# The first FFN's up products: nine of 22 pairs by seven half-size products each

## The chip, the cores and the metric

The kernel runs on one core of one Trainium2 chip. The metric is device microseconds of one launch, from the inputs in HBM to the output in HBM, as the median of several runs.

## The reference

A decoder trunk of two layers works on 512 tokens of width 1024 in float32. Layer 0 mixes the tokens by gated linear attention, layer 1 by a short gated convolution, and each is followed by a convolutional FFN:

```
def conv_ffn(h, w_up, conv_w, w_down):
    up = causal_dwconv(h @ w_up, conv_w)          # (512, 1024) @ (1024, 5632), 3 taps
    a, u = up[..., :D_FF], up[..., D_FF:]         # D_FF = 2816
    return (jax.nn.silu(a) * u) @ w_down          # (512, 2816) @ (2816, 1024)
for i in range(2):
    x = x + mixer_i(rmsnorm(x, norm_mix_g[i]))
    x = x + conv_ffn(rmsnorm(x, norm_ffn_g[i]), w_up[i], conv_w[i], w_down[i])
return rmsnorm(x, final_norm_g)
```

Only the FFN of layer 0 is touched by the change.

## The kernel before, in words

Activations lie transposed: channels on the 128 partitions, 512 tokens along the free axis. `x[0]` to `x[7]` are the residual stream, 128 channels each. Every float32 product is made of three matmuls in the reduced format fp32r: a value is split into a high part (a rounding copy) and a low part (the rest), and `mm3` (L267) multiplies high by high, high by low and low by high into one PSUM bank. The activation's parts are `xparts[k]`; the weight's parts are made on the way in.

Weights come through class `Weights` (L80). A source of 128 x 1024 is loaded by SyncE into one of 4 raw slots (`wraw`). `part` (L151) splits it by `halve` (L118) into one of 3 slots `wh`, `wl`: ScalarE copies the high part, VectorE subtracts it. `take` (L179) is called once per weight unit; it starts a load, lets `part` prepare the unit two ahead, and returns the one that is due. `group` (L274) takes units and runs 24 matmuls for an up unit of 1024 columns.

The program is written with a tile framework which places instructions on each engine's queue at build time and inserts the waits.

The first FFN is `ffn_blocks(0, 1, 2)` (L649). It goes through `ff_steps` (L196). An up step `("up", j)` computes channel block j of the `a` half and of the `u` half (two groups of 24 matmuls of 512 columns), multiplies each by the row factor `r` (L676), applies the three-tap convolution (`conv3`, L328: one ScalarE scaling and two shifted VectorE multiply-adds), SiLU on `a`, the product (L679) and a split into `gp[j]` (L680). The 22 blocks are cut into four (`BLOCKS`: 6, 5, 5 and 6). From the second block on, an up step is followed by one or two down products of the block before, `("dn", b, m)`: 15 or 18 matmuls of 512 columns, added to `x[m]` on VectorE (L656). The eight down products of the last block come at the end. Step 0 also makes `r` (sums of squares, a root, and a reciprocal on VectorE, L325).

The list `SEVEN` (L31) names up steps that are done by Strassen's method in Winograd's form: the pair of channel blocks, the two halves of the 1024 inputs and the two halves of the tokens make a 2 x 2 times 2 x 2 block product, which takes seven half-size products instead of eight. It is empty, so that none of `sums`, `forms`, `seven_forms` (L592), `product` (L608) and `up_seven` (L616) is run. `seven_forms` makes the four sums of activation blocks for one of four pairs of tiles; where `SEVEN` is not empty it runs after steps 1 to 4.

Of the kernel before, what the change touches and what calls it, by code (L numbers as in the profile page):

```python
# [11 lines left out]
F32R = mybir.dt.float32r  # L12
AF = mybir.ActivationFunctionType
ALU = mybir.AluOpType

P = 128
T = 512
D = 1024
KD = D // P
# [8 lines left out]
WARM = 10  # L28
DOWN_CUTS = ((0, 8), (8, 16), (16, 22))
BLOCKS = ((0, 6), (6, 11), (11, 16), (16, 22))  # L30
SEVEN = ()  # L31


@with_exitstack
def trunk_kernel(ctx, tc, xT, w_qk, w_v, w_g, w_up_gate, b_gate, w_go, w_sc, w_so, w_up, w_dn,
# [2 lines left out]
    V, S, G, PE = nc.vector, nc.scalar, nc.gpsimd, nc.tensor  # L38

    const = ctx.enter_context(tc.tile_pool(name="const", bufs=1))  # L40
    wraw = ctx.enter_context(tc.tile_pool(name="wraw", bufs=4))
    wsp = ctx.enter_context(tc.tile_pool(name="wsp", bufs=3))
    work = ctx.enter_context(tc.tile_pool(name="work", bufs=2))
    big = ctx.enter_context(tc.tile_pool(name="big", bufs=1))
    tiny = ctx.enter_context(tc.tile_pool(name="tiny", bufs=2))
# [2 lines left out]
    def ps(name):  # L48
        return psp.tile([P, T], F32, tag="ps", name=name)
# [8 lines left out]
    def bt(tag, name, shape=(P, T), dt=F32):  # L58
        return big.tile(list(shape), dt, tag=tag, name=name)
# [20 lines left out]
    class Weights:  # L80
# [13 lines left out]
            self.units.append(None)  # L94

        def add_pair(self, a, b):
            n, i = len(self.srcs), len(self.units)
            self.srcs += [a, b]
            self.paired.add(n + 1)
            self.last += [i + 3, i + 2]  # L100
            self.need += [n + 1] * 4
            self.units += [(n, q) for q in range(4)]

        def load(self, between=lambda: None):
            if self.nl < len(self.srcs):
                src = self.srcs[self.nl]
                r = wraw.tile([P, UNIT], F32, tag="wraw", name=f"wr{self.nl}")
                n = src.shape[1]
                step = (UNIT // 4, UNIT // 2, UNIT)[min(self.nl, 2)]
                for c in range(0, n, step):  # L110
                    nc.sync.dma_start(r[:, c:min(c + step, n)], src[:, c:min(c + step, n)])
                    between()
                self.raw[self.nl] = r[:, :n]
                self.nl += 1
                if self.nl - 1 in self.paired:
                    self.sums(self.nl - 2)

        def halve(self, hh, ll, src):  # L118
            S.copy(hh, src)  # L119
            V.tensor_sub(ll, src, hh.bitcast(F32))  # L120

        def sums(self, n):

            ra, rb = self.raw[n], self.raw[n + 1]
            lo, hi = slice(0, T), slice(T, 2 * T)
            s = bt(f"b13{'hl'[self.npair % 2]}", f"s{n}")
            self.npair += 1
            nc.sync.dma_start(s, self.srcs[n + 1][:, lo])
            G.dma_start(rb[:, lo], rb[:, hi], accum_op=ALU.add)
            G.dma_start(s, ra[:, lo], accum_op=ALU.add)  # L130
            self.third[n] = s

        def forms(self, n, q, h, l):


            ra, rb = self.raw[n], self.raw[n + 1]
            lo, hi = slice(0, T), slice(T, 2 * T)
            if q == 0:
                self.halve(h[:, lo], l[:, lo], ra[:, lo])
                G.dma_start(ra[:, lo], rb[:, lo], accum_op=ALU.add)  # L140
                self.halve(h[:, hi], l[:, hi], self.third.pop(n))
            elif q == 1:
                self.halve(h[:, hi], l[:, hi], ra[:, hi])
                G.dma_start(ra[:, hi], ra[:, lo], accum_op=ALU.add)
                self.halve(h[:, lo], l[:, lo], ra[:, lo])
            elif q == 2:
                self.halve(h, l, rb)
            else:
                self.halve(h[:, lo], l[:, lo], ra[:, hi])

        def part(self):  # L151
            if self.ns < len(self.units):
                while self.nl <= self.need[self.ns]:
                    self.load()
                tiles = self.hold.pop(self.ns, lambda: None)()
                pair = self.units[self.ns]
                if not tiles:
                    h = wsp.tile([P, UNIT], F32R, tag="wh", name=f"wh{self.ns}")
                    l = wsp.tile([P, UNIT], F32R, tag="wl", name=f"wl{self.ns}")
                if pair:  # L160
                    self.forms(pair[0], pair[1], h, l)
                    self.split[self.ns] = (h, l)
                    self.ns += 1
                    return
                r = self.raw.pop(self.need[self.ns])
                n = r.shape[1]
                whole = 8 <= self.ns < 16
                step = UNIT // 2 if tiles else (UNIT // 4, UNIT // 2, UNIT)[min(self.ns, 2)]
                blocks = []
                for i, c in enumerate(range(0, n, step)):  # L170
                    e = min(c + step, n)
                    hh, ll = tiles[i] if tiles else (h[:, c:e], l[:, c:e])
                    hh, ll = hh[:, :e - c], ll[:, :e - c]
                    self.halve(hh, ll, r[:, c:e])
                    blocks += [(hh[:, b:b + P], ll[:, b:b + P]) for b in range(0, e - c, P)]
                self.split[self.ns] = (h, l) if whole else blocks
                self.ns += 1

        def take(self):  # L179

            for _ in range(2):
                if self.nl < len(self.srcs) and (self.nl < 4 or self.last[self.nl - 4] < self.ns):
                    self.load()
                    if self.nl not in self.paired:
                        break
            self.part()
            self.ng += 1
            return self.split.pop(self.ng - 1)
# [7 lines left out]
    def ff_steps():  # L196
        steps = [("up", j) for j in range(*BLOCKS[0])]
        for b in range(1, len(BLOCKS)):
            n = BLOCKS[b][1] - BLOCKS[b][0]
            for i, j in enumerate(range(*BLOCKS[b])):  # L200
                steps.append(("up", j))
                steps += [("dn", b - 1, m) for m in range(KD * i // n, KD * (i + 1) // n)]
        return steps + [("dn", len(BLOCKS) - 1, m) for m in range(KD)]

    for st in ff_steps():
        if st[0] == "dn":
            a, b = BLOCKS[st[1]]
            W.add(w_dn[0, st[2]][:, a * P:b * P])
        elif st[1] in SEVEN:
            W.add_pair(w_up[0, 2 * st[1]], w_up[0, 2 * st[1] + 1])  # L210
        else:
            W.add(w_up[0, 2 * st[1]])
            W.add(w_up[0, 2 * st[1] + 1])
# [399 lines left out]
                PE.matmul(out, lhsT=a, rhs=b, start=first and k == 0 and i == 0, stop=k == 3 and i == 2,  # L613
                          skip_group_check=not first)

    def up_seven(j, tf):  # L616

        lo, hi = slice(0, HT), slice(HT, T)
        cut = lambda ks, c: [tuple(p[:, c] for p in xparts[k]) for k in ks]
        b11, b21, b22 = cut(range(4), lo), cut(range(4, 8), lo), cut(range(4, 8), hi)  # L620
        t1, t2, t3, t4 = tf
        half = lambda w, c: (w[0][:, c * T:(c + 1) * T], w[1][:, c * T:(c + 1) * T])
        n = "hl"[j % 2]
        sa, sb = bt(f"b11{n}", "sa"), bt(f"b12{n}", "sb")
        A, C = ps("upa")[:, 0:HT], ps("upc")[:, 0:HT]
        w = take()
        product(A, half(w, 0), b11, True)
        S.copy(sa[:, lo], A)
        product(C, half(w, 1), t3, True)
        S.copy(sa[:, hi], C)  # L630
        w = take()
        product(A, half(w, 0), t2, False)
        S.copy(sb[:, lo], A)
        B = ps("upb")[:, 0:HT]
        product(B, half(w, 1), b21, True)
        w = take()
        product(A, half(w, 0), t1, False)
        S.copy(sb[:, hi], A)
        product(C, half(w, 1), t4, False)
        w = take()  # L640
        product(A, half(w, 0), b22, False)
        us = [wk("u", bufs=3) for _ in range(2)]
        V.tensor_add(us[0][:, lo], sa[:, lo], B)
        V.tensor_sub(us[1][:, lo], C, sb[:, lo])
        V.tensor_sub(us[1][:, hi], sa[:, hi], sb[:, hi])
        S.copy(us[0][:, hi], A)
        return us

    def ffn_blocks(l, gi, gnext):  # L649
        gp, r, tf = {}, None, [[], [], [], []]  # L650
        V.tensor_scalar_mul(neg, vec[:, gi * KD:(gi + 1) * KD], -1.0)
        for st in ff_steps():
# [6 lines left out]
                    norm_squares(m)  # L659
                continue  # L660
            j = st[1]
            if j in SEVEN:
                us = up_seven(j, tf)
                for u in us:
                    V.tensor_mul(u, u, r)
            else:
                ups = [group("up0", xparts)]
                if j == 0:
                    sums = sum_parts(acc[0])
                ups.append(group("up1", xparts))  # L670
                if j == 0:
                    r = inv_rms_rows(sums, D)
                    y = wk("y", tag="acc", bufs=1)
                us = [wk("u", bufs=3) for _ in range(2)]
                for u, up in zip(us, ups):
                    V.tensor_mul(u, up, r)  # L676
# [165 lines left out]
```

## Time and profile before

| | |
|---|---|
| median of 3 runs (range) | 1117.98 us (1117.41 to 1118.01) |
| the profiled execution | 1118.37 us, of which the span is 1116.6 us |
| busy: PE, weight load | 1107.2 us (99%), 921.7 us (83%) |
| busy: VectorE, ScalarE, GpSimd | 695.6 us (62%), 460.8 us (41%), 5.1 us |
| granted TensorE clock, mean | 0.997 |
| instructions on PE, VectorE, ScalarE | 5020, 887, 618 |
| HBM traffic | 105.23 MB read, 2.10 MB written |
| first FFN in the span | 211.1 to 570.6 us |

The profile is one execution of the program, taken by the hardware profiler. Its times count from the start of the span. PE is TensorE's matmuls, PEld its weight loads, DVE VectorE, ACT ScalarE, POOL GpSimd, SP SyncE. Matmuls overlap in the pipeline, so that the duration of one is longer than the step from one to the next; what one costs is read from a piece of many. Durations on DVE also reach a little over the start of the next instruction.

### The profile page before, as it was taken

The numbers are of one execution on the slowest core, as the hardware profiler recorded it, in microseconds if no ns is written. First come the engines' busy times: TensorE is split into PE (matmuls) and PEld (weight loads), VectorE is DVE, ScalarE is ACT, GpSimd is POOL, SyncE is SP. The second block draws the span as 40 slices with busy tenths as digits, with TensorE's granted clock in tenths as the row PEclk, the third lists the DMA queues.
The fourth block names the chain that finished last, engine by engine and source line by source line (L and its number), as shares of the span: only waits on it lengthen the run. The fifth ranks groups of instructions, "written<-read, shape, count | busy, mean of one in ns | idle before, by whom it ended". The sixth has DMA issues, their size and how long they took to land.

```text
span 1116.6 us, 12578 instructions
## 1 busy us (share of the span) xinstructions
PE 1107.2 (99%) x5020; PEld 921.7 (83%) x5020; DVE 695.6 (62%) x887; ACT 460.8 (41%) x618; POOL 5.1 (0%) x18
## 2 busy tenths in 40 slices
PE   9999999999999999999999999999999999999997
PEld 7888888888888888888888888888888888888887
DVE  7864675597656566556666555558777777743232
ACT  6565664454333333333442222334444444432241
POOL 1000000000000000000000000000000000000000
PEclk9999999999999999999999999999999999999998
DMA  7232213222332233232332222223332222333312
GB/s 251 83 102 69 73 60 114 95 95 85 98 96 93 92 96 104 90 112 81 108 118 94 95 94 95 95 95 96 101 105 95 95 95 95 90 104 87 102 52 76
DMA packets 34334, 108.14 MB, mean 97 GB/s; under 512 B 3746, under 2 KB 6562, under 8 KB 34276
## 3 DMA queue, kind: packets, MB, share of 16 engines
q1 hardware_dynamic: 34276, 107.34, 29.8%
q8 instruction: 39, 0.64, 0.2%
q14 instruction: 19, 0.16, 0.0%
HBM read 105.23 MB, written 2.10 MB: 96 GB/s over the span
## 4 chain that ended last, share of the span: by engine, by line
PE 99%; DMA 0%; DVE 0%; ACT 0%; SPq 0%; issue 0%; DVEq 0%
PE up L272 43%; PE dn L272 20%; PE g L272 4%; PE v L272 4%; PE so L272 4%; PE scb L272 4%; PE scc L272 4%; PE scu L272 4%; PE go L272 4%; PE k L272 2%; PE q L272 2%; PE dn7b L272 1%; PE dn7a L272 1%; PE o L493 1%; PE o L495 0%; DMA x<-in_xT 0%
## 5 line engine op out<-in xcount | busy, mean ns | idle before, releaser
L119 ACT CAST wh<-wr 128x1024 fp32r<-128x1024 f32 (+4 forms) x209 | 206.3, 988 | 409.3 <-PE up L272 120.6
L120 DVE TENSOR_TENSOR wl<-wr,wh 128x1024 fp32r<-128x1024 f32 (+4 forms) x209 | 238.8, 1143 | 96.0 <-ACT wh L119 94.3
L272 PE MATMUL up<-xh,wh 128*128 128x512 f32 x704 | 273.9, 389 | 0.0
L272 PE MATMUL up<-xl,wh 128*128 128x512 f32 x704 | 273.9, 389 | 0.0
L272 PE MATMUL up<-xh,wl 128*128 128x512 f32 x704 | 273.9, 389 | 0.0
L272 PEld LDWEIGHTS up<-xh,wh 128*128 128x128 f32 x704 | 132.1, 188 | 27.7
L272 PEld LDWEIGHTS up<-xh,wl 128*128 128x128 f32 x704 | 132.1, 188 | 27.3
L272 PEld LDWEIGHTS up<-xl,wh 128*128 128x128 f32 x704 | 132.1, 188 | 27.3
L676 DVE TENSOR_TENSOR u<-up,r 128x512 f32<-128x512 f32 x44 | 30.2, 690 | 90.5 <-PE up L272 90.5
L333 DVE SCALAR_TENSOR_TENSOR c<-u,ffcw,c 128x510 f32<-128x510 f32 x88 | 65.7, 749 | 2.8
L332 DVE SCALAR_TENSOR_TENSOR c<-u,ffcw,c 128x511 f32<-128x511 f32 x88 | 65.3, 745 | 1.1 <-ACT c L331 0.8
L331 ACT ACTIVATE c<-u,ffcw 128x512 f32<-128x512 f32 x88 | 63.0, 720 | 4.1 <-DVE u L676 3.4
L585 DVE TENSOR_TENSOR u<-up,r 128x512 f32<-128x512 f32 x44 | 30.1, 687 | 37.3 <-PE up L272 37.2
L656 DVE TENSOR_TENSOR x<-x,dn 128x512 f32<-128x512 f32 x32 | 21.9, 684 | 16.9 <-PE dn L272 16.9
L587 ACT ACTIVATE c<-c 128x512 f32<-128x512 f32 x22 | 13.9, 632 | 41.9 <-DVE c L333 41.9
L325 DVE RECIPROCAL r<-r 128x512 f32<-128x512 f32 x8 | 26.8, 3351 | 4.7 <-ACT r L324 4.7
L678 ACT ACTIVATE c<-c 128x512 f32<-128x512 f32 x22 | 13.9, 632 | 37.7 <-DVE c L333 37.6
L308 ACT ACTIVATE sq<-x 128x512 f32<-128x512 f32 x34 | 21.0, 624 | 12.6 <-DVE x L716 10.9
L272 PE MATMUL g<-xh,wh 128*128 128x512 f32 x64 | 25.6, 400 | 0.0
L272 PE MATMUL v<-wh,xh 128*128 128x512 f32 x64 | 25.3, 395 | 0.0
L272 PE MATMUL g<-xh,wl 128*128 128x512 f32 x64 | 25.0, 390 | 0.0
L272 PE MATMUL v<-wh,xl 128*128 128x512 f32 x64 | 24.9, 390 | 0.0
(803 smaller groups left out, 1933.5 us busy)
## 6 DMA issues: line engine op xcount, KB each, us to landing
wr<-in_w_up SPq DMA_DIRECT2D x88, 512.0 KB, 3.3
wr<-in_w_sc SPq DMA_DIRECT2D x24, 512.0 KB, 3.3
wr<-in_w_dn SPq DMA_DIRECT2D x24, 384.0 KB, 3.0
wr<-in_w_dn SPq DMA_DIRECT2D x16, 512.0 KB, 3.5
wr<-in_w_dn SPq DMA_DIRECT2D x16, 320.0 KB, 2.8
wr<-in_w_v SPq DMA_DIRECT2D x8, 512.0 KB, 3.4
wr<-in_w_g SPq DMA_DIRECT2D x8, 512.0 KB, 3.4
wr<-in_w_go SPq DMA_DIRECT2D x8, 512.0 KB, 3.3
```

The costliest lines, as they stand in the source:

```text
L119: S.copy(hh, src)
L120: V.tensor_sub(ll, src, hh.bitcast(F32))
L272: PE.matmul(out, lhsT=a, rhs=b, start=first and i == 0, stop=last and i == 2)
L308: S.activation(sq, x[k], AF.Square)
L325: V.reciprocal(r, r)
L331: S.activation(c, u, AF.Copy, scale=cw[:, 2:3])
L332: V.scalar_tensor_tensor(c[:, 1:], u[:, :T - 1], cw[:, 1:2], c[:, 1:], op0=ALU.mult, op1=ALU.add)
L333: V.scalar_tensor_tensor(c[:, 2:], u[:, :T - 2], cw[:, 0:1], c[:, 2:], op0=ALU.mult, op1=ALU.add)
L585: V.tensor_mul(u, ups[i], r)
L587: S.activation(cs[0], cs[0], AF.Silu)
L656: V.tensor_add(x[m], x[m], part)
L676: V.tensor_mul(u, up, r)
```

## The change

`SEVEN` becomes nine of the 22 steps: 7, 9, 10, 12, 14, 15, 17, 19 and 21. Such a step is cut in two, `("s1", j)` and `("s2", j)`, with the first of its down products between them, the others (none or one) behind. `seven_first` runs four of the products (units q0 and q1 of the pair), `seven_last` three (q2 and q3). Each product is 12 matmuls (4 weight blocks, 3 terms) of 256 columns. Two PSUM banks hold them by halves; sums that several outputs share are accumulated in place, and three ScalarE copies and five VectorE operations of 256 columns make the two outputs.

The weight sums were meant for GpSimd's accumulating DMA; they are now four VectorE additions of 512 columns, in `forms`, between the splits of q0 and q1. A pair's weights stay in two raw slots from q0 to q3, a sum in `b13`, and q2's parts in tiles of their own (`b11`, `b12`). There are 6 raw slots instead of 4, and 4 slots of `wh`, `wl` instead of 3. The scratch memory for DMA descriptors is set to 1024.

```
-SEVEN = ()
+SEVEN = (7, 9, 10, 12, 14, 15, 17, 19, 21)
...
-    wraw = ctx.enter_context(tc.tile_pool(name="wraw", bufs=4))
-    wsp = ctx.enter_context(tc.tile_pool(name="wsp", bufs=3))
+    wraw = ctx.enter_context(tc.tile_pool(name="wraw", bufs=6))
+    wsp = ctx.enter_context(tc.tile_pool(name="wsp", bufs=4))
...
             if q == 0:
-                self.halve(h[:, lo], l[:, lo], ra[:, lo])
-                G.dma_start(ra[:, lo], rb[:, lo], accum_op=ALU.add)
-                self.halve(h[:, hi], l[:, hi], self.third.pop(n))
+                s3 = bt(f"b13{'hl'[n % 4 // 2]}", f"s{n}")
+                V.tensor_add(s3, ra[:, lo], rb[:, lo])
+                self.halve(h[:, lo], l[:, lo], s3)
+                V.tensor_add(rb[:, lo], rb[:, lo], rb[:, hi])
+                self.halve(h[:, hi], l[:, hi], rb[:, lo])
             elif q == 1:
-                self.halve(h[:, hi], l[:, hi], ra[:, hi])
-                G.dma_start(ra[:, hi], ra[:, lo], accum_op=ALU.add)
-                self.halve(h[:, lo], l[:, lo], ra[:, lo])
+                self.halve(h, l, ra)
+                V.tensor_add(ra[:, lo], ra[:, lo], rb[:, lo])
+                V.tensor_add(ra[:, hi], ra[:, hi], ra[:, lo])
             elif q == 2:
-                self.halve(h, l, rb)
+                self.halve(h, l, rb[:, hi])
             else:
-                self.halve(h[:, lo], l[:, lo], ra[:, hi])
+                self.halve(h, l, ra)
...
-                if self.nl < len(self.srcs) and (self.nl < 4 or self.last[self.nl - 4] < self.ns):
+                if self.nl < len(self.srcs) and (self.nl < 6 or self.last[self.nl - 6] < self.ns):
...
-                steps.append(("up", j))
-                steps += [("dn", b - 1, m) for m in range(KD * i // n, KD * (i + 1) // n)]
+                dn = [("dn", b - 1, m) for m in range(KD * i // n, KD * (i + 1) // n)]
+                steps += [("s1", j), dn[0], ("s2", j)] + dn[1:] if j in SEVEN else [("up", j)] + dn
...
+    def seven_first(tf):
+
+        dc, ab = ps("updc"), ps("upab")
+        w1, w2 = halves(take())
+        product(dc[:, lo], w1, tf[2], True)
+        product(dc[:, hi], w2, tf[0], False)
         us = [wk("u", bufs=3) for _ in range(2)]
+        e = wk("e7", (P, HT), bufs=1)
+        S.copy(e, dc[:, hi])
+        V.tensor_sub(e, dc[:, lo], e)
+        w1, w2 = halves(take())
+        product(ab[:, lo], w1, cut(range(4), lo), True)
+        product(ab[:, hi], w2, cut(range(4, 8), lo), False)
+        S.copy(us[0][:, lo], ab[:, hi])
+        V.tensor_add(us[0][:, lo], us[0][:, lo], ab[:, lo])
+        return dc, ab, e, us
+
+    def seven_last(dc, ab, e, us, tf):
+        product(dc[:, lo], halves(take())[0], tf[3], False)
+        w2, w1 = halves(take())
+        product(dc[:, hi], w1, cut(range(4, 8), hi), False)
+        product(ab[:, lo], w2, tf[1], False)
+        S.copy(us[0][:, hi], ab[:, lo])
+        V.tensor_sub(us[1][:, lo], dc[:, lo], us[0][:, hi])
+        V.tensor_sub(us[1][:, hi], e, us[0][:, hi])
+        V.tensor_add(us[0][:, hi], dc[:, hi], us[0][:, hi])
         return us
...
-    nc = _bacc.Bacc("TRN2", target_bir_lowering=False, num_devices=1)
+    nc = _bacc.Bacc("TRN2", target_bir_lowering=False, num_devices=1, dynamic_dma_scratch_size=1024)
```

## Rows read from the trace of the kernel before

**Rows 1.** The page: engines by busy time, and the chain that ended last.
```profile
PE 1107.2 (99%) x5020; PEld 921.7 (83%) x5020; DVE 695.6 (62%) x887; ACT 460.8 (41%) x618; POOL 5.1 (0%) x18
...
PE 99%; DMA 0%; DVE 0%; ACT 0%; SPq 0%; issue 0%; DVEq 0%
```

**Rows 2.** Waits of PE: us in total, times, longest.
```profile
PE q L272 <- DVE xl L298: 0.2, 1, 0.2
```

**Rows 3.** Chain in order of time: start us, us, what.
```profile
211.06 10.88 PE up L272 x48
...
374.71 3.40 PE dn L272 x15
...
1089.62 7.91 PE dn7a L272 x66
```

**Rows 4.** Windows: each engine's busy us (instructions), clock, DMA share, GB/s.
```profile
222.00:233.00 11.00, 11.00 (x50) 9.12 (x49) 9.36 (x9) 5.47 (x7) 0.00 (x0) 1.00 0.26 86
233.00:244.00 11.00, 11.00 (x51) 9.09 (x50) 10.03 (x15) 7.26 (x11) 0.00 (x0) 1.00 0.24 88
...
211.00:287.67 76.67, 76.67 (x340) 63.49 (x339) 56.73 (x70) 36.03 (x47) 0.00 (x0) 1.00 0.28 91
...
287.67:531.00 243.33, 243.33 (x1076) 201.47 (x1075) 149.38 (x194) 85.86 (x113) 0.00 (x0) 1.00 0.31 95
```

**Rows 5.** Groups of DVE by form, 290 to 531: busy, mean ns | idle before.
```profile
L120 DVE TENSOR_TENSOR wl<-wr,wh 128x1024 fp32r<-128x1024 f32 x28 | 34.3, 1224 | 4.0 <-ACT wh L119 3.7
...
L676 DVE TENSOR_TENSOR u<-up,r 128x512 f32<-128x512 f32 x29 | 20.1, 692 | 80.5 <-PE up L272 80.5
```

**Rows 6.** Timeline of DVE about step 19: start us, us, instruction [idle before].
```profile
504.59 0.74 DVE L332 SCALAR_TENSOR_TENSOR c<-u,ffcw,c 128x511 f32<-128x511 f32 x1
505.37 0.75 DVE L333 SCALAR_TENSOR_TENSOR c<-u,ffcw,c 128x510 f32<-128x510 f32 x1
506.04 0.68 DVE L656 TENSOR_TENSOR x<-x,dn 128x512 f32<-128x512 f32 x1
506.63 0.68 DVE L679 TENSOR_TENSOR c<-c,c 128x512 f32<-128x512 f32 x1
507.24 0.82 DVE L120 TENSOR_TENSOR wl<-wr,wh 128x640 fp32r<-128x640 f32 x1
...
511.43 0.69 DVE L676 TENSOR_TENSOR u<-up,r 128x512 f32<-128x512 f32 x1 [2.73 <-PE up L272]
```

**Rows 7.** Timeline of DVE in the last stage, 256 columns.
```profile
1097.57 0.42 DVE L728 TENSOR_TENSOR x<-x,dn7a 128x256 f32<-128x256 f32 x1 [5.83 <-PE dn7a L272]
1098.02 0.42 DVE L730 TENSOR_TENSOR sq<-x 128x256 f32<-128x256 f32 x1
```

**Rows 8.** Timeline of DVE in block 0.
```profile
238.53 1.22 DVE L120 TENSOR_TENSOR wl<-wr,wh 128x1024 fp32r<-128x1024 f32 x1
239.67 0.69 DVE L679 TENSOR_TENSOR c<-c,c 128x512 f32<-128x512 f32 x1
```

**Rows 9.** Timeline of ACT, casts of 256 and of 512 columns.
```profile
7.04 0.39 ACT L119 CAST wh<-wr 128x256 fp32r<-128x256 f32 x1
...
507.35 0.62 ACT L287 CAST g19h<-c 128x512 fp32r<-128x512 f32 x1 [0.86 <-DVE c L679]
```

**Rows 10.** Timeline of DVE after the last up pair.
```profile
531.15 0.69 DVE L676 TENSOR_TENSOR u<-up,r 128x512 f32<-128x512 f32 x1 [2.42 <-PE up L272]
...
536.31 0.69 DVE L288 TENSOR_TENSOR g21l<-c,g21h 128x512 fp32r<-128x512 f32 x1
```

**Rows 11.** Timeline of PE near the start.
```profile
11.68 0.39 PE L272 MATMUL q<-xh,wh 128*128 128x512 f32 x1
11.91 0.39 PE L353 MATMUL al<-xh,alsl 128*128 128x512 f32 x1
12.14 0.39 PE L272 MATMUL q<-xl,wh 128*128 128x512 f32 x1
```

**Rows 12.** The page: DMA issues, KB each, us to landing.
```profile
wr<-in_w_up SPq DMA_DIRECT2D x88, 512.0 KB, 3.3
```

More of the change, by code (lines that the diff above doesn't have):

```diff
@@ L96, in add_pair, with end_pair @@
         def add_pair(self, a, b):
-            n, i = len(self.srcs), len(self.units)
+            n = len(self.srcs)
             self.srcs += [a, b]
             self.paired.add(n + 1)
-            self.last += [i + 3, i + 2]
-            self.need += [n + 1] * 4
-            self.units += [(n, q) for q in range(4)]
+            self.last += [None, None]
+            self.need += [n + 1] * 2
+            self.units += [(n, 0), (n, 1)]
+            return n
+        def end_pair(self, n):
+            self.need += [n + 1] * 2
+            self.units += [(n, 2), (n, 3)]
+            self.last[n:n + 2] = len(self.units) - 1, len(self.units) - 2
         def load(self, between=lambda: None):
@@ L114, in load @@
                 self.nl += 1
-                if self.nl - 1 in self.paired:
-                    self.sums(self.nl - 2)
         def halve(self, hh, ll, src):
@@ L120, in halve @@
             V.tensor_sub(ll, src, hh.bitcast(F32))
[L122 to L131, printed above, removed]
         def forms(self, n, q, h, l):
@@ L156, in part @@
                 pair = self.units[self.ns]
-                if not tiles:
+                if pair and pair[1] == 2:
+                    n = "hl"[pair[0] % 4 // 2]
+                    h, l = bt(f"b11{n}", f"wh{self.ns}", dt=F32R), bt(f"b12{n}", f"wl{self.ns}", dt=F32R)
+                elif not tiles:
                     h = wsp.tile([P, UNIT], F32R, tag="wh", name=f"wh{self.ns}")
@@ L208, in trunk_kernel @@
             W.add(w_dn[0, st[2]][:, a * P:b * P])
-        elif st[1] in SEVEN:
-            W.add_pair(w_up[0, 2 * st[1]], w_up[0, 2 * st[1] + 1])
+        elif st[0] == "s1":
+            pair = W.add_pair(w_up[0, 2 * st[1]], w_up[0, 2 * st[1] + 1])
+        elif st[0] == "s2":
+            W.end_pair(pair)
         else:
@@ L614, in product @@
                           skip_group_check=not first)
[L616 to L641, printed above, removed]
-        us = [wk("u", bufs=3) for _ in range(2)]
[L643 to L646, printed above, removed]
@@ new lines, in trunk_kernel, with halves, cut @@
+    lo, hi = slice(0, T // 2), slice(T // 2, T)
+    def halves(w):
+        return [(w[0][:, c:c + T], w[1][:, c:c + T]) for c in range(0, w[0].shape[1], T)]
+    def cut(ks, c):
+        return [tuple(p[:, c] for p in xparts[k]) for k in ks]
+    def seven_first(tf):
[3 more added lines that the diff above has]
+        product(dc[:, hi], w2, tf[0], False)
+        us = [wk("u", bufs=3) for _ in range(2)]
+        e = wk("e7", (P, HT), bufs=1)
[7 more added lines that the diff above has]
+        return dc, ab, e, us
@@ L661, in ffn_blocks @@
             j = st[1]
-            if j in SEVEN:
-                us = up_seven(j, tf)
+            if st[0] == "s1":
+                begun = seven_first(tf)
+                continue
+            if st[0] == "s2":
+                us = seven_last(*begun, tf)
                 for u in us:
```

## The prediction

> **What bounds the kernel now.** I read the page's engine table and its chain first: PE is busy 99% of a 1116.6 us span and PE alone is 99% of the chain that ended last [rows 1]. Next the waits of PE: four lines in all, 3.3 us together, at the program's start and end, the last of them shown; in between PE waits for nobody [rows 2]. So time leaves this kernel only as PE work, and comes back only as PE waits. Then the chain in order of time: an up pair is one piece of 10.88 us with 48 matmuls of 512 columns, 226.7 ns each; a down product over five blocks is 15 of the same, 3.40 us [rows 3], over six 18, which makes 4.08. Last the windows, for what VectorE (DVE) has left: 56.7 us busy of 76.7 while block 0's six up pairs run, 149.4 of 243.3 from there to the end of the last up pair, clock 1.00 throughout [rows 4].
>
> **PE's part of the change.** A changed pair is 7 products x 4 weight blocks x 3 terms = 84 matmuls of 256 columns instead of 48 of 512. The kernel has 256-column matmuls already, in its very last down product: 66 in 7.91 us, 119.8 ns each [rows 3], on the same tile shapes, weights and number format. That is 6.5 ns more than half of 226.7. 84 x 0.1198 = 10.07 us against 10.88: 0.81 us saved per pair, 7.3 us in nine. That is the whole gain there is; bounds from the row: 113.3 ns (exactly half) would give 12.2 us, and 125 ns (5% above the row) 3.4 us. I take the row.
>
> [...]
>
> **What DVE gets.** Prices [rows 5 to 7]: 1024 columns 1.22 us, 512 columns 0.69, a shifted multiply-add 0.75, 256 columns 0.42. In a full queue instructions start sooner than their durations say: 0.60 apart for 512 columns (506.04 to 506.63, 506.63 to 507.24), 0.78 and 0.67 for the two multiply-adds of a convolution [rows 6], 0.45 for 256 [rows 7], 1.14 for 1024 (238.53 to 239.67) [rows 8].
> An up pair now: 2 halvings of 1024, 2 scalings by r, 4 multiply-adds, a product and its split: 2 x 1.22 + 2 x 0.69 + 4 x 0.75 + 2 x 0.69 = 8.2 us by durations, 7.6 by starts.
> A changed pair: 3 halvings of 512 and 2 of 1024, 4 weight sums of 512, 5 output sums of 256, then the same 8 of 512: 3 x 0.69 + 2 x 1.22 + 4 x 0.69 + 5 x 0.42 + 2 x 0.69 + 4 x 0.75 + 2 x 0.69 = 15.1 us by durations, 14.1 by starts. So +6.9 us a pair, 62 in nine.
> A down product: 0.82 + 0.68 = 1.5 by durations, 1.37 by starts (640 columns) [rows 6]; with 768 some 0.1 more, by columns between 640 and 1024.
> The x sums at j = 1 to 4: 4 of 256 and 2 of 512, 4 x 0.42 + 2 x 0.69 = 3.1 us each (3.0 by starts), 12 in all.
> Over up and down together DVE goes from 206 us to 281 of 313, 90% by durations; with the nearly 400 instructions some 0.08 us closer, 80%. It stays below PE on average; the question is each step.
>
> **Where it is hidden.** Take the steps by starts, DVE against PE. A changed pair with two downs of 640 (j = 12, 14, 15): 14.1 + 2.7 = 16.9 against 10.07 + 6.8 = 16.9, a tie. The last, 21, is the same. With two of 768 (7, 9, 10): 17.1 against 18.2. With one down (17, 19): 15.5 against 13.5, DVE 2.0 short. An unchanged pair with one down: 9.0 against 14.3, 5.3 to spare, and one stands next to every short or tied step. The spare time is visible: DVE stands idle 2.73 us before a u and does nothing for PE in it [rows 6]. Can it be used ahead? A weight unit is prepared two takes early and now has 4 slots instead of 3, so q0 and q1 of a pair (4 halvings of 512 or their like and 4 sums, 4.8 us) may be made while the unchanged pair's up products run. The order on DVE is not that of the code: x<-x,dn at 506.04 stands before the c product at 506.63, though its group is later in the program [rows 6]. So ready work fills such gaps. For 9 and 10, the hardest neighbours, I followed the queue by hand: at the start of 9 DVE has q0 and is finishing the epilogue of 8, is free of it 3 us later, owes until the end of 9's products (13.5 us) 0.6 + 1.1 + 2 x 0.45 + 0.9 + 1.2 + 4.8 = 9.5 (q2, q3, two sums, the next down's halving, two x sums, 10's q0 and q1), and so has 10's first units ready some 5 us before PE wants them. I put the nine steps at +0.3 us; bounds 0 and the slow rival below.
>
> The reads of the two shared banks (e and the first half of us[0]) have the down product as cover: the last one starts when q1's products end and PE returns to that bank after the down and two products, 3.4 + 2.9 = 6.3 us later, against an ACT copy of 256 columns (0.39 [rows 9], there to SBUF from SBUF; 0.62 for 512 is its upper bound) and one 256-column sum. Free while DVE is under 5 us late; without that cover PE would wait about 0.9 us a pair.
>
> **Block 0.** There PE has no downs: 10.88 us a step against DVE's 7.6 + 3.0 = 10.6 by starts, 11.3 by durations, for four steps, on top of the lateness that the reciprocal leaves (9.4 and 10.0 us busy of 11 in the windows from 222 to 244 [rows 4]). The halving for the seventh unit ran from 238.53 to 239.7 [rows 8], PE took that unit at 244.15 (211.06 + 6 x 5.44 + 0.45 for the sums): 4.4 us of cover, and a slot more now. By durations four steps lose 4 x 0.4 = 1.5 us. I take +0.8; bounds 0 and 4.
>
> **The last pair, 21.** Its g is wanted by the first down of the last block. Before, that down came behind two others: 6.8 + 15 x 0.2267 = 10.2 us after the up products. Now one has gone into the middle of the pair: 6.8 us. The way to g took from 531.15 to 536.31 + 0.69, 5.9 us [rows 10], and now gets longer, since both outputs end on the last product: one ACT copy 0.4, three sums 1.35, one more scaling 0.6, one more convolution half hidden, 0.7: some 8 to 9. So it is 1 to 3 us late, unless PE's list has work of the next down there. That can be: at the program's start an al matmul stands between two q matmuls that the code issues together [rows 11], so the list follows readiness. I take +0.8; bounds 0 and 3.
>
> **At nothing:** weight loads (same bytes, 3.3 us to land [rows 12], two raw slots more), ACT (some 3 us more a changed pair, beside PE, 85.9 of 243.3 busy [rows 4]), the smaller DMA scratch (no GpSimd DMA is issued on either side), the deeper pools elsewhere (PE waits for nothing there). If a load's cover went, a step would lose at most its 3.3 us.
>
> **Sum.** The profiled execution took 1118.37, 1.8 beyond its span and 0.4 above the median of 1117.98. 1118.37 - 7.3 + 0.8 + 0.8 + 0.3 = 1113.0; against the median 1112.6.
>
> **Rivals.**
> 1. *The margins go together.* Block 0 and pair 21 at their far ends (4 + 3 us) eat nearly all: 1117.98 - 7.3 + 7 = 1117.7; half of it 1114. For it: DVE has 0.3 us to spare a step in block 0. Against: the queue held 4.4 us in its worst moment. Chance of an end between 1115.7 and 1120.2: 0.18.
> 2. *DVE becomes the bound in the changed steps; slower.* Place: DVE's queue between two takes. If nothing is carried over from the unchanged pairs and instructions cost their durations, the steps lose 15.1 + 1.5 - 13.5 = 3.1 us (17 and 19), 15.1 + 3.0 - 16.9 = 1.2 (four), 15.1 + 3.2 - 18.2 = 0.1 (three): 11.3 us, so 1122.0. It gets worse when the sums wait in the queue for ACT's casts: q0 sums, is cast, and is subtracted, twice, and two copies of 256: 2 x 0.62 + 2 x 0.39 = 2.0 us a pair, 18 more, 1140 at the far end. It decides once DVE loses over 0.8 us a changed pair. For it: the ties above; against: the idle time beside each, and an order that fills it. 0.16.
> [...]
> 3. *A half-width matmul costs half.* 113.3 ns, 12.2 us saved: 1117.98 - 12.2 = 1105.8, 1107.7 with the waits of the sum. Against it stand 66 matmuls in one piece at 119.8. 0.03.
> [...]
> The forecast, gain mostly kept, 1110.3 to 1115.7: 0.63.
>
> **How the numbers follow.** 0.2% is 2.2 us, about what a measurement of this kernel can tell from no change. Faster than 1115.7: 0.63 + 0.03 = 0.66; within: 0.18; slower: 0.16. The floor is 1117.98 - 7.3 = 1110.7, and 0.5 for the matmul's price: 1110.2. Upward the range takes rival 1 and the beginning of rival 2, to 1121; about 0.15 is left out. The likeliest case alone is 1110.3 to 1115.7.
>
> **What would show it.** A piece of 84 matmuls in the chain, split by a down into 5.75 and 4.31 us; 119.8 ns right or wrong at once. PE's waits: new lines for wl or us in changed pairs (rival 2), for wl before 290 us or for g21 after the last pair (rival 1). DVE near 281 us busy over the stretch. I am wrong if PE waits over 5 us in all, or if 256 columns cost over 125 ns while DVE is this busy.

## The result

The changed kernel takes 1112.11 us (1111.36 to 1112.38, 4 runs) against 1117.74 (1117.41 to 1118.01, 4 runs): ratio 0.9949, 95% interval 0.9931 to 0.9966. The prediction was 1112.6 us. The profiled execution took 1112.06 us, 1110.0 of it the span, 6.6 us less than before.

The page after: engines by busy time, and the chain by engine (as [rows 1]).

```profile
PE 1100.6 (99%) x5344; PEld 931.3 (84%) x5344; DVE 754.6 (68%) x1019; ACT 488.9 (44%) x688; POOL 5.1 (0%) x18
...
PE 99%; DMA 0%; DVE 0%; ACT 0%; SPq 0%; issue 0%; DVEq 0%
```

PE runs 324 matmuls more in 6.6 us less; DVE is 59 us busier. The waits of PE after, all of them (total us, times, longest; as [rows 2]):

```profile
PE warm L75 <- DVE warm L63: 1.5, 1, 1.5
PE sums L744 <- DVE sq L738: 1.0, 1, 1.0
PE rb L757 <- DVE rl L751: 0.6, 1, 0.6
PE q L273 <- DVE xl L299: 0.2, 1, 0.2
```

They are the four of before: the change has brought PE no wait. The chain in order of time around the first changed pair, step 7 (start, us; as [rows 3]), and its last piece in the first FFN:

```profile
291.78 2.87 PE updc L614 x24
294.65 2.88 PE upab L614 x24
297.53 4.11 PE dn L273 x18
301.64 2.87 PE updc L614 x24
304.51 1.44 PE upab L614 x12
305.95 4.11 PE dn L273 x18
...
527.67 36.35 PE dn L273 x159
564.02 5.44 PE scc L273 x24
```

The pair's 84 matmuls take 2.87 + 2.88 + 2.87 + 1.44 = 10.06 us, 119.8 ns each, against 10.88 before. A piece of 512-column matmuls behind one of 256 takes 0.03 us more than before (4.11 for 18, against 4.08 by [rows 3]'s rate). The FFN began at 211.06 before and at 211.09 now, and its last down product ended at 570.55 and at 564.02: 6.56 us, the whole difference of the spans. The windows (as [rows 4]):

```profile
233.00:244.00 11.00, 11.00 (x50) 9.11 (x49) 11.00 (x17) 7.31 (x11) 0.00 (x0) 1.00 0.24 77
244.00:255.00 11.00, 11.00 (x50) 9.11 (x49) 11.00 (x18) 7.06 (x12) 0.00 (x0) 1.00 0.32 104
255.00:266.00 11.00, 11.00 (x50) 9.10 (x49) 11.00 (x19) 6.38 (x10) 0.00 (x0) 1.00 0.32 89
...
211.00:287.70 76.70, 76.70 (x340) 63.55 (x339) 68.73 (x100) 43.91 (x65) 0.00 (x0) 1.00 0.25 80
287.70:527.67 239.97, 239.97 (x1414) 213.98 (x1414) 194.93 (x292) 106.06 (x163) 0.00 (x0) 1.00 0.33 100
```

In block 0 DVE has become busy without a gap from 233 to 266 us, and PE does not notice; from block 1 to the last pair it is busy 81%.

### The profile page after: what moved, and what is told of

The parts are those of the page before. It is cut to its first block, busy times and chain, and to the rows that moved or that the text cites. A ratio compares the mean times of both kernels' runs of the same rounds, so it can differ in the third digit from the quotient of the medians.

```text
span 1110.0 us, 13420 instructions
## 1 busy us (share of the span) xinstructions
PE 1100.6 (99%) x5344; PEld 931.3 (84%) x5344; DVE 754.6 (68%) x1019; ACT 488.9 (44%) x688; POOL 5.1 (0%) x18
## 4 chain that ended last, share of the span: by engine, by line
PE 99%; DMA 0%; DVE 0%; ACT 0%; SPq 0%; issue 0%; DVEq 0%
PE up L273 34%; PE dn L273 20%; PE updc L614 5%; PE g L273 4%; PE v L273 4%; PE scb L273 4%; PE scu L273 4%; PE scc L273 4%; PE go L273 4%; PE so L273 4%; PE upab L614 4%; PE k L273 2%; PE q L273 2%; PE dn7b L273 1%; PE dn7a L273 1%; PE o L494 1%
## 5 line engine op out<-in xcount | busy, mean ns | idle before, releaser
L124 ACT CAST wh<-wr 128x1024 fp32r<-128x1024 f32 (+4 forms) x227 | 217.0, 957 | 356.1 <-issue 88.3
L125 DVE TENSOR_TENSOR wl<-wr,wh 128x1024 fp32r<-128x1024 f32 (+4 forms) x227 | 250.4, 1106 | 107.8 <-ACT wh L124 106.3
L273 PE MATMUL up<-xh,wh 128*128 128x512 f32 x560 | 217.9, 389 | 0.0
L273 PE MATMUL up<-xl,wh 128*128 128x512 f32 x560 | 217.9, 389 | 0.0
L273 PE MATMUL up<-xh,wl 128*128 128x512 f32 x560 | 217.8, 389 | 0.0
L273 PEld LDWEIGHTS up<-xl,wh 128*128 128x128 f32 x560 | 105.1, 188 | 21.8
L273 PEld LDWEIGHTS up<-xh,wh 128*128 128x128 f32 x560 | 105.1, 188 | 21.8
L273 PEld LDWEIGHTS up<-xh,wl 128*128 128x128 f32 x560 | 105.1, 188 | 21.6
L332 ACT ACTIVATE c<-u,ffcw 128x512 f32<-128x512 f32 x88 | 62.1, 720 | 19.2 <-DVE u L673 11.8
L586 DVE TENSOR_TENSOR u<-up,r 128x512 f32<-128x512 f32 x44 | 30.1, 688 | 37.7 <-PE up L273 37.6
L273 PE MATMUL v<-wl,xh 128*128 128x512 f32 x64 | 24.9, 389 | 0.0
```

The costliest lines, as they stand in the source:

```text
L273: PE.matmul(out, lhsT=a, rhs=b, start=first and i == 0, stop=last and i == 2)
L332: S.activation(c, u, AF.Copy, scale=cw[:, 2:3])
L586: V.tensor_mul(u, ups[i], r)
```

## The experiments

Ten kernels. The theory was that PE's columns set the time and that DVE's work is carried by its neighbours' idle time; the rivals, that the pools bring the gain, that the middle down is needed, and that DVE is close to being the bound. Each time below is the median of four runs or more; before ran beside them at 1117.4 to 1117.8 us.

**Pools alone.**

```
-SEVEN = (7, 9, 10, 12, 14, 15, 17, 19, 21)
+SEVEN = ()
```

> The changed kernel with an empty list of changed pairs: only the deeper pools (6 raw slots, 4 split slots) and the small DMA scratch are left of the change. My theory, that the gain is PE columns alone: no pair is done by sevens, so 1117.7 us, within 0.6 of before, and PE's four waits as before. The rival, that the deeper pools bring part of the gain: under 1116 us.

1117.84 us, ratio to before 0.9999 (0.9989 to 1.0009). The deeper pools and the smaller scratch do nothing by themselves.

**Sixteen pairs.**

```
-SEVEN = (7, 9, 10, 12, 14, 15, 17, 19, 21)
+SEVEN = tuple(range(6, 22))
```

> All sixteen pairs of steps 6 to 21 by sevens. PE alone would save 16 x 0.76 = 12.2 us, 1105.6. My theory, that DVE's limit is its rate from start to start: DVE needs 16 x 14.1 + 24 x 1.4 = 259 us against PE's 16 x 10.1 + 8 x 4.08 + 16 x 3.40 = 249, so PE waits for DVE some 10 us and the time is near 1116. Rival A, that DVE's limit is the sum of its durations: 16 x 15.1 + 24 x 1.53 = 278, 29 over, near 1134. Rival B, that DVE is far from any limit: 1105.6 with no wait of PE.

1105.38 us, ratio 0.9886 (0.9871 to 0.9901): rival B's time, and the best version of this study. PE's waits are the four of before, 3.3 us in all. The window from 287.70 to the last pair, and three pieces of the chain in the first half of step 21, where the list has put three matmuls for `upab` between those for `updc`, so that PE has no gap there:

```profile
287.70:521.65 233.95, 233.95 (x1635) 219.74 (x1635) 227.66 (x370) 121.93 (x201) 0.00 (x0) 1.00 0.31 99
```

```profile
508.15 1.68 PE updc L614 x14
509.83 0.36 PE upab L614 x3
510.19 1.20 PE updc L614 x10
```

DVE is busy 227.7 of 234 us, 97%, so rival B has the time right and the reason wrong: a limit is very near, only my price of DVE was too high. The prediction's 0.45 [rows 7] and 0.78 [rows 6] were steps from an instruction to one that reads what it wrote; where the list puts other work between the two, the step is shorter. From the changed kernel's DVE timeline (start, us):

```profile
340.85 0.42 DVE L649 TENSOR_TENSOR u<-updc,u 128x256 f32<-128x256 f32 x1
341.19 0.41 DVE L650 TENSOR_TENSOR u<-e,u 128x256 f32<-128x256 f32 x1
341.64 0.42 DVE L651 TENSOR_TENSOR u<-updc,u 128x256 f32<-128x256 f32 x1
341.98 1.28 DVE L673 TENSOR_TENSOR u<-u,r 128x512 f32<-128x512 f32 x2
343.34 0.69 DVE L661 TENSOR_TENSOR x<-x,dn 128x512 f32<-128x512 f32 x1
343.94 1.41 DVE L333 SCALAR_TENSOR_TENSOR c<-u,ffcw,c 128x511 f32<-128x511 f32 x2
345.27 1.41 DVE L334 SCALAR_TENSOR_TENSOR c<-u,ffcw,c 128x510 f32<-128x510 f32 x2
```

256 columns are 0.34 apart, and 0.45 only before L651, which overwrites what L650 reads (the prediction had 0.45 for all). Two multiply-adds, those of `a` and of `u` in turn, take 1.33, 0.66 each (it had 0.78 and 0.67). That makes a pair 13.3 us instead of 14.1.

**No down product in the middle.**

```
-steps += [("s1", j), dn[0], ("s2", j)] + dn[1:] if j in SEVEN else [("up", j)] + dn
+steps += [("s1", j), ("s2", j)] + dn if j in SEVEN else [("up", j)] + dn
```

> Nine pairs as in the changed kernel, but the two halves of a pair follow each other and all its down products come behind. The prediction priced the lost cover of the bank reads at 0.9 us a pair: 9 x 0.9 = 8 us, 1120. The theory that I hold now: from the last read of a bank to PE's return to it there are still two products of 256 columns, 2.9 us, which cover a copy and a sum of 0.8 us wherever DVE is not over 2 us late; then 1112 to 1114, and any wait of PE shows on the first product of a second half.

1112.06 us, the changed kernel's 1112.11. With nine pairs the middle down buys nothing; the prediction's "0.9 us a pair without that cover" had overlooked the two products that still lie between.

**Four more DVE instructions a pair.**

```
+for _ in range(4):
+    V.tensor_add(s3, ra[:, lo], rb[:, lo])
 V.tensor_add(s3, ra[:, lo], rb[:, lo])
```

> The changed kernel with the first weight sum of each pair computed five times instead of once: four more VectorE instructions of 512 columns a pair, 2.8 us by durations, 2.4 by starts. My theory (unchanged neighbours lend their spare time, DVE stays below PE over the stretch): PE waits under 3 us in all, 1112 to 1115. The rival (each changed step stands for itself and was already a tie): 9 x 2.4 = 22 us more, 1134.

1111.47 us, no wait of PE in the changed pairs. 9 x 2.4 = 22 us of DVE work more cost nothing: a tie in one step is no limit where its neighbours have time.

**The pools of before, nine pairs.**

```
-    wraw = ctx.enter_context(tc.tile_pool(name="wraw", bufs=6))
-    wsp = ctx.enter_context(tc.tile_pool(name="wsp", bufs=4))
+    wraw = ctx.enter_context(tc.tile_pool(name="wraw", bufs=4))
+    wsp = ctx.enter_context(tc.tile_pool(name="wsp", bufs=3))
...
-                if self.nl < len(self.srcs) and (self.nl < 6 or self.last[self.nl - 6] < self.ns):
+                if self.nl < len(self.srcs) and (self.nl < 4 or self.last[self.nl - 4] < self.ns):
```

> The nine changed pairs with the pools of before: 4 raw slots and 3 split slots (the load condition looks 4 back again). The prediction hid DVE's work of a changed pair in its neighbours by the fourth split slot. If that slot, or the two raw ones, carry the work over, PE waits 5 us or more without them, in changed pairs and for g21 behind the last pair: 1117 or slower. If at nine pairs DVE has so much idle time that two units ahead are enough: 1112, within 1 us of the changed kernel.

1111.31 us. Two units ahead in three slots were enough for nine pairs; the fourth slot was not what carried the work.

**Sixteen pairs without the middle down** (both diffs above).

> All sixteen pairs of steps 6 to 21 by sevens, no down product in the middle. With sixteen DVE was busy some 98% of the stretch, so that its queue is late. If the 2.9 us of PE work that are left between a bank's reads and PE's return are enough cover even then: 1105 to 1107. If the middle down is what makes sixteen possible, PE waits for e or us about 0.9 us a pair: 1120. In between, 1107 to 1112, with waits of PE on DVE in single pairs.

1111.81 us, 6.4 above sixteen with it: the case in between. The wait on the bank's reader is there, in two pairs and not in all, nearly the whole of it in step 21; then the chain's piece behind it (start, us):

```profile
PE updc L614 <- DVE e L635: 2.6, 2, 2.4
```

```profile
518.44 4.61 PE updc L614 x24
```

3.0 us of new waits are named, and PE's busy time is 4 us above sixteen's for the same 5596 matmuls. A part of that is the clock: behind the wait of 2.4 us, 24 matmuls take 4.61 us instead of 2.87, at a granted clock of 0.50 from 520 to 522 us. Where the other 2 us of busy time lie was not settled.

**Sixteen pairs, two more DVE instructions each** (the loop of four above, with two).

> Sixteen pairs with the first weight sum of each computed three times: two more VectorE instructions of 512 columns a pair. My theory now: DVE's price in a full queue is its duration less 0.08 us, 0.60 for 512 columns, 0.34 for 256, 1.14 for 1024, 0.66 for a multiply-add, so 13.3 us a pair and 1.34 to 1.47 a down; sixteen pairs need 245 of PE's 250 us, and with 16 x 2 x 0.60 = 19 more 264, 14 over: PE waits for DVE 10 to 16 us and the time is 1116 to 1121. The rival, that even this is hidden (the limit is elsewhere): 1105 to 1107. By durations, 16 x 2 x 0.69 = 22 more on a DVE that would have been over already: 1127.

1125.05 us: 19.7 above sixteen, for 16 x 2 x 0.60 = 19.2 us of DVE work. The direction was mine, the size not: I had given sixteen pairs 5 us to spare, and there was nothing. DVE's window, and PE's largest new wait:

```profile
287.70:540.70 253.00, 240.74 (x1638) 222.20 (x1637) 247.08 (x402) 122.88 (x204) 0.00 (x0) 0.99 0.29 91
```

```profile
PE dn L275 <- DVE wl L125: 7.1, 5, 2.2
```

DVE is busy 98% of the stretch here, hardly more than with sixteen, and the stretch is longer: DVE is idle for 5.9 us of it, as against 6.3 with sixteen. This is rival 2 of the prediction, real once DVE is full: these 19.2 us of DVE work cost 19.7 us of the kernel. Only this one amount was tried.

**Seventeen pairs.**

```
-steps = [("up", j) for j in range(*BLOCKS[0])]
+steps = [("up", j) for j in range(5)] + [("s1", 5), ("s2", 5)]
...
+SEVEN = tuple(range(5, 22))
```

> Seventeen pairs, steps 5 to 21; step 5 lies in block 0, where no down product is, so that its halves follow each other. PE alone would save 0.76 us more than with sixteen, 1104.6. DVE is busy all the time from 222 to 277 us already with nine pairs, and step 5 adds 6 us to it there. If DVE's lateness in block 0 has no cover left, PE waits up to 6 us: 1106 to 1111. If the two units ahead still cover it: 1104.6.

1110.83 us, 5.5 above sixteen: block 0 has no cover left for one pair more. PE waits there for the last of the x sums and then for `e`, and its clock falls. PE's waits, a piece of the chain (start, us) and windows of PE (clock after the engines' busy times):

```profile
PE updc L614 <- ACT tb3h L288: 1.3, 1, 1.3
...
PE updc L614 <- DVE e L635: 0.9, 1, 0.9
PE updc L614 <- DVE tb3l L289: 0.7, 1, 0.7
```

```profile
272.21 3.36 PE updc L614 x14
```

```profile
270.00:272.20 2.20, 0.38 (x1) 0.19 (x1) 2.20 (x5) 1.39 (x3) 0.00 (x0) 0.95 0.00 0
272.20:275.60 3.40, 3.35 (x14) 3.06 (x14) 2.29 (x3) 0.01 (x1) 0.00 (x0) 0.53 0.30 88
```

The waits make 2.9 us, and the slower clock 1.7 us more in that piece (14 matmuls in 3.36 us instead of 1.68).

**Sixteen pairs with the pools of before** (both diffs above).

> Sixteen pairs with 4 raw slots and 3 split slots, as before the change. With nine pairs the old pools cost nothing (1111.3 us). DVE is full with sixteen, so that a weight unit which may start one unit later leaves it idle where it has no time to be idle. If the deeper pools are what lets DVE run full: PE waits, 1108 to 1116. If two units ahead suffice here too: 1105 to 1106.

1112.55 us, 7.2 above sixteen. So the deeper pools do matter where DVE is full (raw and split slots were not taken back one by one): PE waits for split weights, 3.3 us in three places, and its clock falls to 0.91 in the window from 480 to 500.

```profile
PE dn L273 <- DVE wl L125: 3.3, 3, 2.5
```

**Seventeen pairs, sums on GpSimd** (`V.tensor_add` to `G.tensor_add` in the four sums of `forms`).

> Seventeen pairs, steps 5 to 21, with the four weight sums of each on GpSimd, which does nothing in this stretch. That takes 4 x 0.60 = 2.4 us a pair from DVE. If what cost the seventeen pairs 5.5 us against the sixteen was DVE's time alone: 1104.6, one PE saving of 0.76 below sixteen. If a GpSimd sum of 512 columns takes well over 1 us or slows DVE beside it, PE waits for split weights in pairs that follow each other: 1107 to 1120.

1139.32 us, 28 us slower than with DVE's sums and beyond both cases of the expectation. PE's new waits are 22.7 us, none of them for split weights; the largest:

```profile
PE updc L614 <- DVE e L635: 7.1, 3, 3.2
```

Groups by form (busy us, mean ns | idle before), first a GpSimd sum and DVE in this kernel:

```profile
L140 POOL TENSOR_TENSOR wr<-wr,wr 128x512 f32<-128x512 f32 x15 | 26.1, 1741 | 21.5 <-DVE wl L125 13.9 <-ACT u L639 5.1 <-ACT g5h L288 2.4
...
L125 DVE TENSOR_TENSOR wl<-wr,wh 128x512 fp32r<-128x512 f32 x29 | 27.8, 964 | 0.1
...
L650 DVE TENSOR_TENSOR u<-e,u 128x256 f32<-128x256 f32 x14 | 11.2, 798 | 0.0
```

and the same DVE groups with sixteen pairs and no GpSimd:

```profile
L125 DVE TENSOR_TENSOR wl<-wr,wh 128x512 fp32r<-128x512 f32 x29 | 19.8, 683 | 0.0
...
L650 DVE TENSOR_TENSOR u<-e,u 128x256 f32<-128x256 f32 x15 | 6.2, 416 | 0.0
```

A sum takes 1.5 to 2.5 us by groups (1.7 in the one shown) where DVE's took 0.69, and the two DVE groups shown, whose inputs are both in SBUF, are stretched: 683 to 964 ns, 416 to 798. Not every such group is (L687 has 680 ns against 683); L649, with one input in PSUM, has 414 against 418. These are means; the timeline (start, us) shows a GpSimd sum, L649 and L650 beside it, and an L650 with no sum beside it:

```profile
317.69 1.89 POOL L141 TENSOR_TENSOR wr<-wr 128x512 f32<-128x512 f32 x1
...
318.35 0.41 DVE L649 TENSOR_TENSOR u<-updc,u 128x256 f32<-128x256 f32 x1
318.68 1.18 DVE L650 TENSOR_TENSOR u<-e,u 128x256 f32<-128x256 f32 x1
...
338.87 0.41 DVE L650 TENSOR_TENSOR u<-e,u 128x256 f32<-128x256 f32 x1
```

So L650 takes 1.18 beside a sum and 0.41 without one (the same in all 17 of this kernel: 7 beside a sum, 10 not), and L649, which reads one of its inputs from PSUM, takes 0.41 beside the same sum. DVE's busy time in the first FFN hardly falls (332 us, against 334 with its own sums): what the sums took off it, the stretching gave back. How the 28 us divide between late sums and stretched instructions was not settled.

## Why the prediction was right, and where only two errors met

- **PE's price.** 119.8 ns a matmul was read from the last down product and held to the digit with DVE far busier: 10.06 us a pair for a predicted 10.07, in parts of 5.75 and 4.31 as forecast, 9 x 0.82 = 7.4. Missing was the change of width, twice a pair: 18 x 0.03 = 0.5 us.
- **Waits.** The sum had +0.8 for block 0, +0.8 for pair 21 and +0.3 for the steps, 1.9 in all. Measured: 0, 0.3 and 0. 7.4 - 0.5 - 0.3 = 6.6 is the span's gain; the prediction had 7.3 - 1.9 = 5.4.
- **What was luck.** The medians differ by 5.6 us (1117.74 to 1112.11), the FFN alone by 6.6: the missing 1 us lies outside the changed FFN. The profiled execution of before was 0.6 us above that median, and with the pools alone the first FFN took the same 359.49 us as before in a span 0.9 us shorter. So the forecast of 1112.6 looks nearer (0.5) than its terms were (1.2).
- **Block 0.** The term was mis-sized by its whole 0.8: DVE is busy 11.00 of 11 us for three windows running and PE waits for nothing. Its lateness stayed within the units prepared ahead. (The window that the prediction read for block 0, to 287.67, holds seven up pairs and not six: step 6's come before the first down. Nothing in the sum hangs on it.) Seventeen pairs showed where that cover ends.
- **Pair 21.** Here the mechanism is visible on both sides. PE's timeline after (start, us):

```profile
534.11 0.39 PE L273 MATMUL dn<-g20h,wl 128*128 128x512 f32 x1
534.34 0.39 PE L273 MATMUL dn<-g16h,wh 128*128 128x512 f32 x1
...
537.06 0.39 PE L273 MATMUL dn<-g20h,wh 128*128 128x512 f32 x1
537.36 0.50 PE L273 MATMUL dn<-g21h,wh 128*128 128x512 f32 x1
```

  In the code g21 follows g20 at 534.34. It came at 537.36, 3.0 us late, as the far end of that step had it; but the list placed 13 matmuls of the next down (g16 to g20) in between, and PE lost about 0.3 us at the splice. The same readiness that [rows 11] showed at the program's start worked here.
- **DVE's prices** were too high by 0.8 us a pair, which made ties of steps that had time to spare; with the right ones steps 17 and 19 are still 1.2 us short by themselves. At nine pairs that is worth at most the 0.3 us of the steps, and it is why the expectation for sixteen missed by 10 us. Over the stretch from 211 us to the last pair DVE is busy 264 us (68.7 + 194.9), where the prediction had 281 by durations and 32 less by starts.
- **What hides it.** I named the fourth slot and the middle down. Neither is needed for nine pairs (1111.3 and 1112.1 us without); at sixteen the deeper pools together are worth 7.2 us and the middle down 6.4. What hides nine pairs is the idle time of DVE itself, 45 us between 287.70 and 527.67: another 22 us of work fitted into it. That it takes a list that places ready work to use this time is argued from the orders seen; no run varied the order alone.
- **Rival 1** did not occur: block 0's margin held, and pair 21's did not (3.0 us late), but PE had other work there. **Rival 2** has its point of decision later than priced: not at 0.8 us a step, but where DVE is full over the whole stretch, with sixteen pairs. **Rival 3** is excluded: 119.8 ns, not 113.3.

## What to carry to other kernels

Where PE is the whole chain, count its columns by the measured price of the very shape, including what a change of shape costs (0.03 us each time here), and take the other engine's load over a whole stretch and not step by step: steps lend each other time as far as units are prepared ahead. Ask how far the limit is by adding work to the hidden engine (22 us more were free here with nine pairs, while 19.2 us cost 19.7 with sixteen); then use up the distance, as the sixteen pairs do with 1105.4 us. Buffers and spacing that show no effect under a light load can be worth several us once the hidden engine is full (here the deeper pools 7.2 us and the middle down 6.4 at sixteen pairs, nothing at nine).

## What the runs showed of the hardware

- In the DVE timelines shown, an instruction that does not need the one before starts about 0.08 us before that one's recorded end: after 0.34 us for 256 columns (duration 0.42; 340.85 to 341.19 in the changed kernel), 0.60 for 512 (0.68 [rows 6]), 1.14 for 1024 (1.22 [rows 8]) and 0.66 for a multiply-add (1.33 for two that are recorded with 1.41, 343.94 to 345.27 in the changed kernel). One that reads what the one before wrote starts after its end: 0.45 for 256 columns (duration 0.42 [rows 7]), 0.78 for a multiply-add (0.74 [rows 6]).
- With seventeen pairs and the sums on GpSimd, L650, which reads both inputs from SBUF, took 1.18 us beside a sum and 0.41 without one (256 columns), and L649, which reads one input from PSUM, took 0.41 beside the same sum. What makes the difference was not shown.
- With seventeen pairs PE did 0.38 us of work in 2.2 us (270.00 to 272.20), and the granted clock of the next window was 0.53: its 256-column matmuls were 0.21 us apart (272.81 to 275.15 us in eleven steps) instead of 0.12. To the 2.0 us of waits there (1.3 and 0.7) these matmuls added 1.7 us, 3.36 for 14 instead of 1.68.
